# Gated DeltaNet layer of a two-layer backbone: the delta rule's scans issued in one order with both directions side by side, Q S in a PSUM bank of its own, 1/|k|² as a factor of a product, and the inverses' copies shared by two engines

## The chip, the cores and the metric

The kernel runs on one core of one Trainium2 chip. The metric is the device time of one execution in microseconds, the median of the runs shown. The kernel before took 1455.19 us (three runs, 1454.19 to 1458.78).

## The reference, cut to what matters

The network has two layers over 512 tokens (256 of context, 256 latent) of width 1024: a latent-attention layer with a SwiGLU channel mixer, then a bidirectional gated DeltaNet layer with a SwiGLU channel mixer. The change lies in the DeltaNet layer. Per value head and direction it computes, chunk by chunk:

```python
diff = gcum[..., :, None] - gcum[..., None, :]
decay = jnp.where(incl, jnp.exp(jnp.where(incl, diff, 0.0)), 0.0)
kb = kc * bc[..., None]
lmat = jnp.where(strict, jnp.einsum('bhnid,bhnjd->bhnij', kb, kc) * decay, 0.0)
a = lmat + jnp.eye(CHUNK, dtype=f32)
...
sol = lax.linalg.triangular_solve(a, rhs, left_side=True, lower=True, unit_diagonal=True)
attn = jnp.einsum('bhnid,bhnjd->bhnij', qc, kc) * decay
...
def step(S, inp):
    w_i, u_i, qd_i, kd_i, a_i, gl_i = inp
    v_new = u_i - jnp.einsum('bhck,bhkv->bhcv', w_i, S)
    o_i = jnp.einsum('bhck,bhkv->bhcv', qd_i, S) + jnp.einsum('bhij,bhjv->bhiv', a_i, v_new)
    S = S * gl_i[..., None, None] + jnp.einsum('bhck,bhcv->bhkv', kd_i, v_new)
    return S, o_i
```

The keys are divided by their norm before this. Both directions run over the context first and then over the latent tokens; only the latent output is used in this last layer.

## The kernel before, in words

**Work units.** The function `gdn` (L831) does the DeltaNet mixer. A unit n (0 to 7) is one key head with its two value heads e; a group g is two units. Tokens are cut into four chunks of 128 (0 and 1 context, 2 and 3 latent). The two directions d visit them in the orders (0, 1, 2, 3) and (1, 0, 3, 2).

**Steps.** `GDN_STEPS` (L71) is a hand-written table of some 70 words in which the steps are recorded: `keys`, `queries`, `values`, `gates` (projections from the layer input, streamed weights, a five-tap convolution on VectorE), `base` (the 32x32 diagonal blocks of the triangular matrices are inverted on GpSimd, one group at a time), `decays` and `invert` (one unit's triangular matrices and their inverses), `scan` (one unit's recurrence), `finish` or `last` (norm, gate and transpose of a unit's output) and `out` (the output projection, in parts). A scheduler then orders the instructions of each engine; steps in `URGENT` (L76), scans among them, get priority. An engine works its own list strictly in the order that comes out.

**decays (L1131).** For each direction a tile `N` of eight 128x128 blocks (chunk, value head) is loaded from `g_dram`, masked on GpSimd (L1147) and turned into decays by an Exp on ScalarE with the bias `nb` (L1149). `nb` holds the negative cumulated decay, less the logarithm of |k|²; this logarithm is made in `decay_factors` (L1020 to L1029) by two Newton steps on eight numbers per token row: per group 12 small VectorE instructions on the tiles `lnk`, `lnk_e`, `lnk_d` and `nb`, with two Exps between them. VectorE then multiplies with the products Q K (`at`, L1155, two instructions of 128x512 per unit) and K K (`N`, L1163, two instructions of 128x1024 per unit), both read from PSUM.

**invert (L1167).** The 32x32 inverses come by DMA. TensorE joins them to 64x64 blocks (`T` L1198, `Y` L1209 to L1211) and those to 128x128 (`T` L1220, `Y` L1226). Between the two rounds the results are copied from PSUM into `XA` and `N`: two copies on ScalarE (L1214) and four on VectorE (L1215, L1216); after the second round two on VectorE (L1228).

**scan (L1230).** A loop over four steps t, and in it over the two directions. In each: `ks` = K S (L1254) and, for latent chunks, Q S (L1256) into the other half of the same PSUM bank; `rr` (VectorE, L1259); `pw` = T rr (L1262); `w`, its copy (ScalarE, L1264); K^T w into the second half of the `pw` bank (L1268); the new state `S` (ScalarE at t = 0, VectorE afterwards, L1273); for latent chunks `av` (L1279) and the output `o` (L1284 to L1288). `ks` and `pw` take turns in two PSUM banks, called `ch`. Two further banks, `inv`, belong to decays and invert.

**Weights.** `Stream` loads weight tiles on SyncE's DMA queue (`raw`), splits each into `whi` (ScalarE, L185) and `wlo` (VectorE, L186), and three TensorE instructions use them (L213 to L215). These streamed products (`q`, `k`, `v`, `z`, `out`) are what the scheduler puts between the links of the scans.

Of the kernel before, what the change touches and what calls it, by code (L numbers as in the profile page):

```python
# [11 lines left out]
I32 = mybir.dt.int32  # L12
# [59 lines left out]
for _x in """keys0 base0 queries0 values0 keys1 base1 queries1 decays0 invert0 keys2 values1 decays1 invert1 queries2 gates1 base2 gates0 scan0 decays2 invert2 values2 scan1 scan2 decays3 gates2 invert3 values3 gates4 keys3 gates3 queries3 base3 finish0 scan3 decays4 invert4 gates5 values4 decays5 values5 values6 gates6 invert5 scan4 decays6 finish1 invert6 gates7 scan5 decays7 invert7 values7 out0 finish2 fetch0 scan6 out1 scan7 out2 out3 last6 out4 last7""".split():  # L72
    GDN_STEPS.append((_x[:-1], int(_x[-1])))
# [23 lines left out]
def tile_trunk(ctx: ExitStack, tc: tile.TileContext, xT, params, consts, gconsts, wmod, w0, w1, out):  # L97
# [15 lines left out]
    def bank(name="bank", tag="bank"):  # L113
        tags = env["tags"]
        if tag not in tags:
            tag = "bank" if "bank" in tags else "pj"
# [714 lines left out]
    def gdn(st, u, head, pool, big, fetch_base):  # L831
# [151 lines left out]
        def keys(g):  # L983
# [17 lines left out]
            ss, rk2 = tl([P, 8], "ss", 2), tl([P, 8], "rk2", 2)  # L1001
# [5 lines left out]
            groups[g] = dict(KT=KT, ss=ss, kk=kk)  # L1007

            def decay_factors():
# [8 lines left out]

                ln, ex, df = (tl([P, 8], n) for n in ("lnk", "lnk_e", "lnk_d"))
                V.tensor_scalar(ln, ss.bitcast(I32), math.log(2.0) / 2 ** 23, -math.log(2.0) * (127 - 0.043), op0=ALU.mult, op1=ALU.add)  # L1020
                for _ in range(2):
                    S.activation(ex, ln, AF.Exp)
                    V.tensor_tensor(df, ss, ex, op=ALU.subtract)
                    V.tensor_tensor(ex, ex, ss, op=ALU.add)
                    V.reciprocal(ex, ex)
                    V.tensor_tensor(df, df, ex, op=ALU.mult)
                    V.scalar_tensor_tensor(ln, df, 2.0, ln, op0=ALU.mult, op1=ALU.add)
                nb, bd = tl([P, 2, 2, 4, 2], "nb", 3), tl([P, 2, 2, 4, 2], "bd", 3)
                V.tensor_tensor(kc(nb), kc(ngc[:, :, gu]), wide(ln), op=ALU.subtract)  # L1029
                groups[g].update(nb=nb, bd=bd)  # L1030
# [67 lines left out]
        def values(n):  # L1098
            g, k = n // 2, n % 2
            s = groups[g]  # L1100
            Kt, Vt = tl([P, 4, P], "Kt", 1), tl([P, 4, 2, P], "Vt", 3)
# [20 lines left out]
            bd, Kb = s["bd"][:, :, k], tl([P, 2, 3, 2, P], "Kb", 2)  # L1122
# [8 lines left out]
        def decays(n):  # L1131
            if "nb" not in groups[n // 2]:
                flush()
            g, k = n // 2, n % 2
            s = groups[g]
            KT, QT, nb = s["KT"][:, k], s["QT"][:, k], s["nb"][:, :, k]
# [5 lines left out]
            for d in range(2):  # L1142
                for i in range(0, 8, 4):
# [4 lines left out]
                    for q in range(i, i + 4):  # L1148
                        S.activation(N[d][:, q], N[d][:, q], AF.Exp, bias=nb[:, d, q // 2, q % 2:q % 2 + 1])  # L1149
# [3 lines left out]
            at = tl([P, 2, 2, 2, P], "at", 2)  # L1153
            for d in range(2):
                V.tensor_tensor(at[:, d], qk[:, 0:TS].rearrange("p (c t) -> p c t", c=2).unsqueeze(2).to_broadcast([P, 2, 2, P]),  # L1155
                                N[d][:, 4:8].rearrange("p (c e) t -> p c e t", c=2), op=ALU.mult)
# [4 lines left out]
            for d in range(2):  # L1161
                x = N[d].rearrange("p (c e) t -> p c e t", e=2)
                V.tensor_tensor(x, kk.rearrange("p (c t) -> p c t", c=4).unsqueeze(2).to_broadcast([P, 4, 2, P]), x, op=ALU.mult)  # L1163
# [3 lines left out]
        def invert(n):  # L1167
# [22 lines left out]

            def qv(p, n):
# [20 lines left out]
            for d in range(2):  # L1212
                a0, b0, a1, b1 = tb[d]
                S.activation(X[B[b0], :, B[a0 % 2]], ps[d][B[b0]], AF.Copy)  # L1214
                V.tensor_copy(N[d][B[a0], :, B[b0]], ps[d][B[a0]])  # L1215
                V.tensor_copy(N[d][B[a1], :, B[b1]], ps[d][B[a1]])  # L1216
# [10 lines left out]
            for d in range(2):  # L1227
                V.tensor_copy(N[d][H[d], :, H[1 - d]], p[H[d]])  # L1228

        def scan(n):  # L1230
# [5 lines left out]
            KT, QT = s["KT"][:, k], s["QT"][:, k]  # L1236
            Sm = [tl([P, 2, P], "S", 4) for d in range(2)]
            o = tl([P, 2, 2, P], "o", 4)
            avb = bank("av", "av")
            av = avb.rearrange("p (c e n) -> p c e n", c=2, e=2)  # L1240
            opened = None
            for t in range(4):
                for d in range(2):
                    c = CHUNKS[d][t]
                    cs = slice(c * P, c * P + P)
                    Sk = Sm[d].rearrange("p e n -> p (e n)")
                    rr = Vt[:, c]

                    def tkn(x, e_):
                        return x[:, d, n, c, e_:e_ + 1]  # L1250

                    if t > 0:
                        ks = bank("ks", "ch")
                        PE.matmul(ks[:, :TS], KT[:, cs], Sk, start=True, stop=True)  # L1254
                        if c >= 2:
                            PE.matmul(ks[:, TS:], QT[:, (c - 2) * P:(c - 2) * P + P], Sk, start=True, stop=True)  # L1256
                        rr = tl([P, 2, P], "rr", 2)
                        for e_ in range(2):
                            V.scalar_tensor_tensor(rr[:, e_], ks[:, e_ * P:e_ * P + P], tkn(neg, e_), Vt[:, c, e_], op0=ALU.mult, op1=ALU.add)  # L1259
                    pw = bank("pw", "ch")  # L1260
                    for e_ in range(2):
                        PE.matmul(pw[:, e_ * P:e_ * P + P], N[d][:, 2 * c + e_], rr[:, e_], start=True, stop=True)  # L1262
                    w = tl([P, 2, P], "w", 3)
                    S.activation(w.rearrange("p e n -> p (e n)"), pw[:, 0:TS], AF.Copy)  # L1264
                    if t < 3:
                        kd = pw[:, TS:]
# [439 lines left out]
```

## Time and profile before

| | us |
|---|---|
| median of three runs | 1455.19 (1454.19 to 1458.78) |
| the profiled execution | 1455.09 |
| its span in the trace | 1453.3 |
| TensorE busy, share of the span | 1354.8 (93%) |
| VectorE busy | 990.0 (68%) |
| ScalarE busy | 734.7 (51%) |
| GpSimd busy | 221.4 (15%) |

The DeltaNet mixer fills the trace from about 695 to 1240 us. Before it lie the first layer and the mixer's first products, behind it the second channel mixer. In the profile's rows, "PE" is TensorE, "PEld" its weight loads, "DVE" VectorE, "ACT" ScalarE, "POOL" GpSimd and "SP" SyncE; "PEclk" is the share of TensorE's full clock that was granted in a stretch. A row of a table by stages reads: stretch, its length, busy time and count of each engine, granted clock, DMA share, GB/s. TensorE's busy time includes the modelled ends of its instructions, so a busy TensorE may still be waiting inside a chain of dependent products.

### The profile page before, as it was taken

What the parts mean: (1) busy time and instruction counts of PE and PEld (TensorE: products, weight loads), DVE (VectorE), ACT (ScalarE), POOL (GpSimd) and SP (SyncE); (2) the same over time, 40 slices, a digit from 0 to 9 for tenths busy, and PEclk for the clock granted to TensorE, in tenths of its full rate; (3) what the DMA queues carried; (4) which work ended last, traced back from release to release, by engine and by line L of the source; (5) the groups of instructions that cost most, each with busy time, mean ns of one, the idle gap of its engine ahead of it and who ended that gap; (6) DMA issues with size and microseconds to landing.
All of it is one profiled execution on the core that took longest, in us unless ns stands there. A gap on an engine that the chain in (4) does not pass through costs nothing. (4 is left out here: it accounts for less than half of the span.)

```text
span 1453.3 us, 27885 instructions
## 1 busy us (share of the span) xinstructions
PE 1354.8 (93%) x10753; PEld 1166.3 (80%) x10753; DVE 990.0 (68%) x2038; ACT 734.7 (51%) x1603; POOL 221.4 (15%) x329
## 2 busy tenths in 40 slices
PE   7999999999999999999797979889998998999996
PEld 4767687769989998987686858777877897899996
DVE  3355566979757956867789977667775765656665
ACT  3434444366524543542647645665566543745542
POOL 0000000050000000000017992934600000000000
PEclk9979999999999999999999989899999998899998
DMA  9444412654423332355146545433343243665551
GB/s 379 145 142 150 129 44 100 227 217 146 130 88 98 120 124 95 122 185 193 46 143 168 163 114 132 134 105 109 92 135 129 71 138 131 195 186 186 182 181 58
DMA packets 131692, 204.75 MB, mean 141 GB/s; under 512 B 70632, under 2 KB 72040, under 8 KB 131432
## 3 DMA queue, kind: packets, MB, share of 16 engines
q1 hardware_dynamic: 129656, 200.90, 43.3%
q10 hardware_dynamic: 1904, 2.08, 0.5%
q8 instruction: 84, 1.38, 0.4%
q14 instruction: 48, 0.39, 0.1%
HBM read 192.92 MB, written 10.03 MB: 140 GB/s over the span
## 5 line engine op out<-in xcount | busy, mean ns | idle before, releaser
L186 DVE TENSOR_TENSOR wlo<-raw,whi 128x512 fp32r<-128x512 f32 x422 | 295.7, 708 | 202.8 <-ACT whi L185 183.6
L185 ACT ACTIVATE whi<-raw 128x512 fp32r<-128x512 f32 x422 | 263.1, 630 | 322.1 <-PE ffo L214 71.5
L214 PE MATMUL ffo<-hidl,whi 128*128 128x512 f32 (+1 forms) x352 | 119.4, 339 | 0.0
L215 PE MATMUL ffo<-hidh,wlo 128*128 128x512 f32 (+1 forms) x352 | 119.2, 339 | 0.0
L213 PE MATMUL ffo<-hidh,whi 128*128 128x512 f32 (+1 forms) x352 | 118.9, 341 | 0.0
L185 ACT ACTIVATE whi<-wsum 128x512 fp32r<-128x512 f32 x88 | 54.9, 630 | 61.0 <-PE x L214 26.2
L1089 POOL TENSOR_TENSOR m<-m,mt 128x31 f32<-128x31 f32 (+15 forms) x124 | 79.1, 638 | 9.2
L1088 POOL TENSOR_TENSOR mt<-m 128x31 f32<-128x31 f32 (+15 forms) x124 | 77.1, 622 | 9.2
L213 PEld LDWEIGHTS ffo<-hidh,whi 128*128 128x128 f32 x352 | 66.9, 190 | 8.4 <-issue 0.7
L214 PEld LDWEIGHTS ffo<-hidl,whi 128*128 128x128 f32 x352 | 66.9, 190 | 8.0 <-issue 0.7
L215 PEld LDWEIGHTS ffo<-hidh,wlo 128*128 128x128 f32 x352 | 66.9, 190 | 7.6
L186 DVE TENSOR_TENSOR wlo<-wsum,whi 128x512 fp32r<-128x512 f32 x88 | 60.1, 689 | 15.8 <-ACT whi L185 15.5
L213 PE MATMUL z<-uhi,whi 128*128 128x256 f32 x216 | 62.9, 291 | 1.7 <-DVE acc L946 1.0
L215 PE MATMUL z<-uhi,wlo 128*128 128x256 f32 x216 | 62.8, 292 | 0.7 <-DVE wlo L186 0.7
L214 PE MATMUL z<-ulo,whi 128*128 128x256 f32 x216 | 61.9, 287 | 0.0
L213 PE MATMUL v<-uhi,whi 128*128 128x512 f32 x128 | 53.4, 417 | 7.3 <-ACT whi L185 4.6
L1177 POOL MEMSET XA<- 128x512 f32 x2 | 1.0, 525 | 364.0 <-PE modps L347 364.0
L1527 POOL TENSOR_TENSOR N<-N,mean 128x256 f32<-128x256 f32 x4 | 2.8, 722 | 332.8 <-DVE rs_t L247 332.8
L215 PE MATMUL v<-uhi,wlo 128*128 128x512 f32 x128 | 52.6, 412 | 0.7 <-DVE wlo L186 0.7
L560 POOL TENSOR_TENSOR r<-r,rstd 128x512 f32<-128x512 f32 x4 | 6.2, 1566 | 301.2 <-ACT rstd L549 300.3
L214 PE MATMUL v<-ulo,whi 128*128 128x512 f32 x128 | 52.0, 406 | 0.0
L213 PE MATMUL x<-t,whi 128*128 128x256 f32 x176 | 49.6, 282 | 0.1
(481 smaller groups left out, 4296.2 us busy)
## 6 DMA issues: line engine op xcount, KB each, us to landing
raw<-in_w_dram SPq DMA_DIRECT2D x153, 512.0 KB, 3.7
mraw<-in_wmod_dram SPq DMA_DIRECT2D x80, 512.0 KB, 5.4
raw<-in_w_dram SPq DMA_DIRECT2D x138, 256.0 KB, 2.9
raw<-in_wmod_dram SPq DMA_DIRECT2D x32, 256.0 KB, 4.5
N<-g_dram SPq DMA_DIRECT2D x16, 512.0 KB, 4.5
x<-in_xT_dram SPq DMA_DIRECT2D x4, 512.0 KB, 10.2
h<-in_xT_dram SPq DMA_DIRECT2D x1, 2048.0 KB, 9.3
m<-g_dram SPq DMA_DIRECT2D x16, 128.0 KB, 4.9
```

What stands on the lines that cost most here:

```text
L185: S.activation(hi, src, AF.Copy)
L186: V.tensor_tensor(lo, src, f32(hi), op=ALU.subtract)
L213: PE.matmul(ps_ap, a[0], b[0], start=first, stop=False, **kw)
L214: PE.matmul(ps_ap, a[0], b[1], start=False, stop=False, **kw)
L215: return PE.matmul(ps_ap, a[1], b[0], start=False, stop=last, **kw)
L560: (V if fb < 4 else G).tensor_tensor(r[fb], r[fb], rs if fb == 0 else f, op=ALU.mult)
L1088: G.tensor_tensor(tv, m[:, 0:j, j:j + 1].to_broadcast([P, j, w]), m[:, j:j + 1, j:32].to_broadcast([P, j, w]), op=ALU.mult)
L1089: G.tensor_tensor(m[:, 0:j, j:32], m[:, 0:j, j:32], tv, op=ALU.subtract)
L1177: G.memset(X, 0.0)
L1527: G.tensor_tensor(res.r[fb], res.r[fb], ms, op=ALU.subtract)
```

## The change

Five things are changed in the DeltaNet mixer; the table of steps is the same.

1. The logarithm of |k|² goes. The Exp takes the cumulated decay alone as its bias, and 1/|k|² (`rk2`, there already) is multiplied in on VectorE together with Q K and K K: `times`, one instruction per direction and chunk. Per unit there are four of 128x256 for `at` and eight for `N`, instead of two of 128x512 and two of 128x1024.
2. Between the rounds of invert, all copies of direction 0 are on VectorE and all of direction 1 on ScalarE.
3. The scan has both directions in each step, half a bank each: both K S into one `ks` bank, both Q S into a bank `qs` of the `inv` pair, then `rr`, `pw` and `w` of both, the state of both, the output of both.
4. Each TensorE instruction of a scan is issued after the one before it in the scan's own text (`mm` with `after(tail[0])`). The helper `fill` would put a step's generator between them; the table names no such step (no word with a "+"), so it does nothing here.
5. More buffers for `rk2`, `Vt`, `Kb`, `rr` and `w`, and a smaller scratch area for dynamic DMAs.

```diff
-                ln, ex, df = (tl([P, 8], n) for n in ("lnk", "lnk_e", "lnk_d"))
-                V.tensor_scalar(ln, ss.bitcast(I32), math.log(2.0) / 2 ** 23, -math.log(2.0) * (127 - 0.043), op0=ALU.mult, op1=ALU.add)
-                for _ in range(2):
-                    S.activation(ex, ln, AF.Exp)
-                    V.tensor_tensor(df, ss, ex, op=ALU.subtract)
-                    V.tensor_tensor(ex, ex, ss, op=ALU.add)
-                    V.reciprocal(ex, ex)
-                    V.tensor_tensor(df, df, ex, op=ALU.mult)
-                    V.scalar_tensor_tensor(ln, df, 2.0, ln, op0=ALU.mult, op1=ALU.add)
...
-                        S.activation(N[d][:, q], N[d][:, q], AF.Exp, bias=nb[:, d, q // 2, q % 2:q % 2 + 1])
+                        S.activation(N[d][:, q], N[d][:, q], AF.Exp, bias=ngc[:, d, n, q // 2, q % 2:q % 2 + 1])
...
+            def times(dst, c, d, x):
+                e2 = N[d][:, 2 * c:2 * c + 2]
+                V.scalar_tensor_tensor(dst, e2, rk2[:, c:c + 1], x.unsqueeze(1).to_broadcast([P, 2, P]), op0=ALU.mult, op1=ALU.mult)
...
+            def copy(d, dst, src):
+                V.tensor_copy(dst, src) if d == 0 else S.activation(dst, src, AF.Copy)
...
-                S.activation(X[B[b0], :, B[a0 % 2]], ps[d][B[b0]], AF.Copy)
-                V.tensor_copy(N[d][B[a0], :, B[b0]], ps[d][B[a0]])
-                V.tensor_copy(N[d][B[a1], :, B[b1]], ps[d][B[a1]])
+                copy(d, X[B[b0], :, B[a0 % 2]], ps[d][B[b0]])
+                copy(d, N[d][B[a0], :, B[b0]], ps[d][B[a0]])
+                copy(d, N[d][B[a1], :, B[b1]], ps[d][B[a1]])
...
+            def mm(*args, **kw):
+                with after(tail[0]):
+                    tail[0] = PE.matmul(*args, **kw)
+                return tail[0]
...
+                if t > 0:
+                    ks = bank("ks", "ch")
+                    for d, c in enumerate(cs):
+                        mm(half(ks, d), KT[:, c * P:c * P + P], Sk[d], start=True, stop=True)
+                    if t >= 2:
+                        qs = bank("qs", "inv")
+                        for d, c in enumerate(cs):
+                            mm(half(qs, d), QT[:, (c - 2) * P:(c - 2) * P + P], Sk[d], start=True, stop=True)
+                    else:
+                        fill()
```

In the scan every TensorE instruction of the changed kernel bears the line of `mm`, L1247. Where the instructions stand now is shown at three places.

VectorE's list before, in front of the copies of unit 0's first joined blocks (`N<-Y`); `lnk` and `nb` are the logarithm of group 1, which unit 0 does not need:

```order
L1174 STREAM_TRANSPOSE xb<-yb 128x256
L1025 RECIPROCAL lnk_e<-lnk_e 128x8
L1026 TENSOR_TENSOR lnk_d<-lnk_d,lnk_e 128x8
L1174 STREAM_TRANSPOSE yb<-xb 128x256
L1027 SCALAR_TENSOR_TENSOR lnk<-lnk_d,lnk 128x8
L1023 TENSOR_TENSOR lnk_d<-ss,lnk_e 128x8
L1024 TENSOR_TENSOR lnk_e<-lnk_e,ss 128x8
L1025 RECIPROCAL lnk_e<-lnk_e 128x8
L1026 TENSOR_TENSOR lnk_d<-lnk_d,lnk_e 128x8
L1027 SCALAR_TENSOR_TENSOR lnk<-lnk_d,lnk 128x8
L1029 TENSOR_TENSOR nb<-ngc,lnk 128x32
L186 TENSOR_TENSOR wlo<-raw,whi 128x512 x2
```

The same place now, with the copies themselves at the end (`rk_8532` is 1/|k|² of group 1):

```order
L1165 STREAM_TRANSPOSE xb<-yb 128x256
L1005 RECIPROCAL rk_8532<-ss 128x8
L1038 COPY ssq<-ss 128x8
L1165 STREAM_TRANSPOSE yb<-xb 128x256
L1020 TENSOR_TENSOR bd<-beta,rk_8532 128x32
L1006 TENSOR_TENSOR kkc<-kkd,rk_8532 128x256
L1183 COPY XA_7342<-Y_8290 32x8x32
L1183 COPY N<-Y_8290 32x8x32 x2
```

The ten rows of the logarithm and two splits of weights no longer stand ahead of the copies, and three copies stand there instead of four.

TensorE's list before, in the last two steps of the last scan (unit 7), where `out` is the streamed output projection:

```order
L1268 MATMUL pw<-w,Kb 128x128 x2
L1279 MATMUL av<-w,at 128x128 x2
L215 MATMUL out<-uhi,wlo 128x256
L1262 MATMUL pw<-rr,N 128x128 x2
L1254 MATMUL ks<-S,KT 128x256
L1256 MATMUL ks<-S,QT 128x256
L1268 MATMUL pw<-w,Kb 128x128 x2
L1279 MATMUL av<-w,at 128x128 x2
L1262 MATMUL pw<-rr,N 128x128 x2
L1254 MATMUL ks<-S,KT 128x256
L1256 MATMUL ks<-S,QT 128x256
```

The last scan now, from its second step on:

```order
L1247 MATMUL ks<-S,KT 128x256 x2
L1247 MATMUL pw<-rr,N 128x128 x4
L1247 MATMUL pw<-w,Kb 128x128 x4
L1247 MATMUL ks<-S,KT 128x256 x2
L1247 MATMUL qs<-S,QT 128x256 x2
L1247 MATMUL pw<-rr,N 128x128 x4
L1247 MATMUL pw<-w,Kb 128x128 x4
L1247 MATMUL av<-w,at 128x128 x4
L1247 MATMUL ks<-S,KT 128x256 x2
L1247 MATMUL qs<-S,QT 128x256 x2
```

The directions no longer alternate, and streamed products no longer stand between the links: from the first to the last `pw` of unit 7 there are 154 instructions of `out` in the list before and 19 now. The rest stands behind the scan: behind the last `pw` come 221 instructions of `out` now, 96 before.

TensorE's list now, where unit 4's `K K` product (`kk`) and its first joining product (`T`, which reads the finished `N`) stand, at the end of scan 3:

```order
L1247 MATMUL pw_10977<-rr_10969,N_9930 128x128 x2
L1151 MATMUL kk_11032<-KT_8384 128x128 x4
L1247 MATMUL av_10878<-w_10975,at_9963 128x128 x2
L1192 MATMUL T32_11055<-xb_11046,N_10992 32x32 x2
L1192 MATMUL T32_11055<-xb_11046,N_10994 32x32 x2
```

Only two products stand between `kk` and `T` now; before, the rows of most of a scan and of streamed `v` products stood between them.

More of the change, by code (lines that the diff above doesn't have):

```diff
@@ L115, in bank @@
         if tag not in tags:
-            tag = "bank" if "bank" in tags else "pj"
+            tag = next(t for t in ("bank", "ch", "pj") if t in tags)
         return env["ps"].tile([P, 512], F32, name=name, tag=tag, bufs=tags[tag])
@@ L1227, in invert, with drain, scan @@
             for d in range(2):
-                V.tensor_copy(N[d][H[d], :, H[1 - d]], p[H[d]])
-        def scan(n):
+                copy(d, N[d][H[d], :, H[1 - d]], p[H[d]])
+        def drain(steps):
+            for _ in steps:
+                pass
+        def scan(n, beside=()):
             if units[n].get("turned") != 1:
@@ L1236, in scan @@
             KT, QT = s["KT"][:, k], s["QT"][:, k]
+            beside, tail = iter(beside), [None]
             Sm = [tl([P, 2, P], "S", 4) for d in range(2)]
+            Sk = [x.rearrange("p e n -> p (e n)") for x in Sm]
             o = tl([P, 2, 2, P], "o", 4)
@@ new lines, in fill, with half, tkn @@
+            def fill():
+                for _ in range(2):
+                    with after(tail[0]):
+                        tail[0] = next(beside, tail[0])
+            def half(x, d):
+                return x[:, d * TS:d * TS + TS]
+            for t in range(4):
+                cs = [CHUNKS[d][t] for d in range(2)]
+                def tkn(x, d, e_):
+                    return x[:, d, n, cs[d], e_:e_ + 1]
+                rr = [Vt[:, c] for c in cs]
+                if t > 0:
[8 more added lines that the diff above has]
+                        fill()
+                    for d, c in enumerate(cs):
+                        rr[d] = tl([P, 2, P], "rr", 4)
@@ new lines, in scan @@
+                if t < 2:
+                    fill()
+                    continue
+                first = t == 2
+                for d, c in enumerate(cs):
+                    for e_ in range(2):
+                        opened = mm(av[:, c - 2, e_], at[:, d, c - 2, e_], ws[d][:, e_], start=opened is None, stop=not first, skip_group_check=True)
+                        q_ = half(qs, d)[:, e_ * P:e_ * P + P]
+                        if first:
+                            S.activation(o[:, c - 2, e_], q_, AF.Copy, scale=tkn(egc, d, e_))
+                        else:
+                            V.scalar_tensor_tensor(o[:, c - 2, e_], q_, tkn(egc, d, e_), o[:, c - 2, e_], op0=ALU.mult, op1=ALU.add)
+                    if not first:
+                        V.tensor_tensor(o[:, c - 2], o[:, c - 2], av[:, c - 2], op=ALU.add)
@@ L1289, in scan @@
+            drain(beside)
             un["o"] = o
@@ L1335, in project @@
                         ins = ob[m // 2][1] = first
+                    yield first
                 if k1 == 16 and m % 2:
@@ L1344, in gates @@
             for i in range(2):
-                ins = product(p[:, i * TS:i * TS + TS], upl, ins)
+                for k, x in enumerate(upl):
+                    with after(ins):
+                        ins = mm3(p[:, i * TS:i * TS + TS], st.take(), x, k == 0, k == NB - 1)
+                    yield ins
+                flush(ins)
             th, zt = tl([P, T], "th", 3), tl([P, 2, TS], "zt", 2)
@@ L1587, in _layer1_blocks @@
     ms = []
-    for step, i in GDN_STEPS:
+    for step, i in (x for steps in GDN_STEPS for x in steps):
         if step == "keys":
```

92 lines of the change are left out of this document (36 added, 56 removed).

## The prediction

> **What bounds the kernel now.** I read the page's first lines, then a table of the mixer by stages, then the waits of TensorE, the timelines at two places, and the groups of VectorE and ScalarE. The page gives the engines' shares of the span of 1453.3 us:
>
> ```profile
> PE 1354.8 (93%) x10753; PEld 1166.3 (80%) x10753; DVE 990.0 (68%) x2038; ACT 734.7 (51%) x1603; POOL 221.4 (15%) x329
> ```
>
> TensorE is the bound on the whole, so only its idle time and its throttled time can be won. By stages (the rows start with stretch and length, then TensorE's busy time, and end with granted clock, DMA share and GB/s):
>
> ```profile
> 840.00:873.00 33.00, 23.37 (x308) 19.59 (x308) 28.75 (x57) 15.32 (x36) 29.93 (x38) 0.84 0.46 111
> 873.00:1007.00 134.00, 121.73 (x1372) 104.30 (x1371) 96.99 (x236) 78.48 (x223) 61.21 (x107) 0.94 0.45 122
> 1007.00:1107.00 100.00, 95.23 (x966) 80.57 (x964) 72.10 (x151) 67.07 (x193) 36.86 (x58) 1.00 0.37 110
> 1107.00:1174.00 67.00, 60.09 (x782) 52.35 (x781) 40.95 (x102) 32.46 (x97) 1.22 (x2) 0.97 0.33 104
> 1174.00:1206.00 32.00, 30.18 (x232) 28.92 (x232) 20.88 (x58) 14.59 (x38) 0.00 (x0) 1.00 0.43 132
> 1206.00:1240.00 34.00, 26.05 (x158) 23.61 (x159) 21.35 (x63) 13.16 (x33) 0.00 (x0) 0.80 0.36 124
> ```
>
> The eight scans run from 873 to 1206. TensorE stands idle there for 12.27 + 4.77 + 6.91 + 1.82 = 25.8 us; no better order of the scans can win more. The stretch in front, with the first inverses (840 to 873), has 9.6 us idle and a clock of 0.84; the tail behind (1206 to 1240) has 8.0 us idle and 0.80. What lies before 695 and behind 1240 is not touched by the change; I put it at 0, give or take 4 us, an estimate, since the scheduler shifts a few products there.
>
> The sum is made against the profiled execution's own 1455.09 us, 0.1 us under the median.
>
> **Part A, the logarithm in front of unit 0's inverse.** The longest single wait of a join in 690 to 870, and VectorE's timeline around it (start, length):
>
> ```profile
> PE T L1220 <- DVE N L1216: 8.0, 1, 8.0
> ```
>
> ```profile
> 849.03 1.63 DVE L1026 TENSOR_TENSOR lnk_d<-lnk_d,lnk_e 128x8 f32<-128x8 f32 x1
> ...
> 855.22 1.76 DVE L186 TENSOR_TENSOR wlo<-raw,whi 128x512 fp32r<-128x512 f32 x2
> 856.91 0.41 DVE L1215 COPY N<-Y 32x256 f32<-32x256 f32 x1
> ```
>
> TensorE waits 8.0 us for copies that are ready to run but stand behind group 1's logarithm and two weight splits. In VectorE's list these rows are gone now. From 849.03 to 855.22 the logarithm takes 6.2 us, with small instructions of up to 1.63 us each in it. The splits (1.76) come later as well, and one of four copies (0.4) goes to ScalarE. Together 8.4 us leave the place, more than the wait, so what is late next there is TensorE's own work: 20 streamed `v` products now stand before `T`, which before mostly stood behind it. Cover used here is missing elsewhere, so I take −6, the logarithm alone; the ends are −8.0 (the whole wait) and −3 (half of the logarithm, if something else ends the wait). TensorE's granted clock was 0.84 over these 33 us, so 0.16 of 33 = 5.3 us of work were lost to the throttle. I leave that out of the sum, since the stretch has other waits than this one.
>
> [...]
>
> The logarithm's other cost is VectorE's time (two tiles of the chain, 690 to 1000; the first figure after the length is VectorE's):
>
> ```profile
> 690.00:1000.00 310.00, 11.52 (x32) 1.63 (x8) 0.93 0.46 124
> 690.00:1000.00 310.00, 4.89 (x16) 1.63 (x8) 0.93 0.46 124
> ```
>
> 16.4 us for 48 instructions; outside unit 0's place it lies beside TensorE's projections, and I count it at 0.
>
> **Part B, the scans.** The timeline inside one scan before:
>
> ```profile
> 1149.86 0.68 PE L1262 MATMUL pw<-rr,N 128*128 128x128 f32 x4
> ...
> 1150.58 0.38 ACT L1264 ACTIVATE w<-pw 128x256 f32<-128x256 f32 x1 [1.33 <-PE pw L1262]
> ...
> 1151.83 0.61 DVE L1273 SCALAR_TENSOR_TENSOR S<-S,egl,pw 128x128 f32<-128x128 f32 x2
> ...
> 1153.07 0.70 PE L1254 MATMUL ks<-S,KT 128*128 128x256 f32 x2
> ...
> 1154.24 0.61 DVE L1259 SCALAR_TENSOR_TENSOR rr<-ks,neg,Vt 128x128 f32<-128x128 f32 x2
> ```
>
> Before, `rr` could start only when Q S had been written into the same bank (1153.07 to 1154.24, 1.17 us); with Q S in its own bank it needs K S alone, 0.70. One direction's loop is `pw` to `w` 0.72, `w` through K^T w to `S` 1.25, `S` 0.61, K S 0.70, `rr` 0.61: 3.9 us, and with both directions in step nothing but this loop need bound a step. The groups (count | busy, mean ns | idle before, and for whom):
>
> ```profile
> L1259 DVE SCALAR_TENSOR_TENSOR rr<-ks,neg,Vt 128x128 f32<-128x128 f32 x96 | 29.1, 345 | 23.2 <-PE ks L1256 15.9 <-PE ks L1254 6.9
> L1163 DVE TENSOR_TENSOR N<-kk,N 128x1024 f32<-128x1024 f32 x16 | 19.1, 1215 | 0.0
> L1228 DVE COPY N<-Y 64x512 f32<-64x512 f32 x16 | 11.0, 686 | 3.2 <-PE Y L1226 3.0
> L1215 DVE COPY N<-Y 32x256 f32<-32x256 f32 x16 | 6.7, 416 | 0.8 <-ACT XA L1214 0.5
> L1288 DVE TENSOR_TENSOR o<-o,av 128x256 f32<-128x256 f32 x16 | 6.7, 416 | 6.7 <-PE av L1279 6.7
> L186 DVE TENSOR_TENSOR wlo<-raw,whi 128x512 fp32r<-128x512 f32 x175 | 126.9, 733 | 69.2 <-ACT whi L185 67.0 <-issue 0.9 <-PE k L214 0.5
> ```
>
> - `rr` waited 15.9 us for Q S. TensorE was busy with streamed products in part of that, so I take half: −8; the ends are 0 and −15.9. TensorE's 25.8 us of idle would hold either.
> - The products in `N` and `at` have 256 columns now. By `o`, of that size, one takes 0.42 us: per unit 8 x 0.42 = 3.4 for `N` in place of 2 x 1.215 = 2.4. (Those in `at` are read by the outputs `av` alone, at the end of a step: 0.) At unit 4 only two small products stand between `kk` and the join that needs `N`, so the 3.4 are open: +3.4. At the other units I take the difference of a quarter of a microsecond at most, +1.6. Together +5; the ends are 0 and 8 x 3.4 = +27, the last if no unit had cover.
> - Q S now takes a bank of the pair that decays and invert use. It may wait until VectorE or ScalarE has emptied `T` or `Y` from it; behind Q S on TensorE stand `pw` of both directions, and all of the scan waits for those. Such a release is one copy away (0.42 to 0.69 us). No row shows this wait; I take 0, between 0 and 24 x 0.69.
> - Copies: VectorE gives up two per unit of 0.42 and one of 0.69 and takes one of 0.42; ScalarE the reverse. Neither is near its limit over the scans (96.99 and 78.48 of 134 us in the first row), so 0. No DMA is added or moved, and SyncE's list is unchanged around the scans.
> - `fill` finds no step to put in, so it costs and brings nothing; the larger buffers allow the two directions' tiles to live at once.
>
> Part B: −8 + 5 = **−3**.
>
> **Part C, the tail.** Times at the end, from the chain of waits: first unit 7's first `pw`, then what follows its last, then (from TensorE's timeline) the first and the last of a run of streamed products between:
>
> ```profile
> 1174.44 0.71 PE pw L1262 x4
> ```
>
> ```profile
> 1203.16 0.76 PE pw L1262 x4
> ...
> 1213.13 0.64 PE oT L1318 x4
> 1215.26 0.74 PE out L213 x4
> ...
> 1222.06 0.43 PE lnmean L493 x2
> ```
>
> ```profile
> 1206.16 0.74 PE L213 MATMUL out<-uhi,whi 128*128 128x256 f32 x4 [1.01 <-ACT uhi L218]
> ...
> 1212.15 0.28 PE L215 MATMUL out<-uhi,wlo 128*128 128x256 f32 x1
> ```
>
> From 1206.16 to 1212.27 stand 48 `out`: 0.127 us each. Scan 7 takes 1174.44 to 1203.16 = 28.7 us from its first `pw` to its last, with 154 `out` in it. Without them the loop of Part B bounds it: 2.6 to the first state, two loops of 3.9, and 1.3 for the last K S and `rr` make 11.7; 0.6 for the second direction behind the first on VectorE, 1.0 for two outputs `o` ahead of an `rr`, and 19 x 0.127 = 2.4 for the `out` that stay make 15.7: −13.0. Ten more `out` stand in front: +1.3. Behind the last `pw`, 221 `out` in place of 96: the last state, `osq`, and the norm up to the transpose took 1203.16 to 1213.13; 145 `out` (18.4 us) cover them all now. Then 67 `out` follow up to the first `lnmean`, and they cover the wait from 1213.13 to 1215.26. So from the last `pw` to `lnmean` 212 x 0.127 + 1.2 for transposes and `av` = 28.1, where it was 1222.06 − 1203.16 = 18.9: +9.2. Sum −2.5. Part of the tail's throttled time (0.80 over 34 us) may go with the waits, −0.5. I take **−3**; the ends are −7 (the whole 8.0 us of idle goes, less the norm's chain behind `lnmean`) and +2 (the links of scan 7 cost 1 us a step more).
>
> **Sum.** 1455.09 − 6 − 3 − 3 = **1443 us**.
>
> **The rivals.**
> - *R1, slower: lockstep scans stand open.* The streamed products were what filled the links; fewer stand inside the later scans now, and VectorE works its list in order, so a weight split (0.733) can stand ahead of each `rr`, with both directions' `pw` behind it. On 24 steps that is 24 x 0.733 = +17.6 in Part B in place of −3. The sum is 1455 − 6 + 17.6 − 3 = 1464. It decides where Part B is over +9, and is measured as slower over +13.4. For it speak that TensorE has no second direction half a step away any more to work on, and that VectorE is 72% busy in the first scans; against it, that products displaced from a scan are not lost but shorten something else. Chance 0.23.
> - *R2, hidden.* The wait of Part A is only moved: VectorE's list gets shorter, but `v` waits for `whi` or its sums there, and scans win and lose alike: A −2, B 0, C 0, 1453. Range 1451 to 1459. Chance 0.18.
> - *R3, more.* All waits for Q S go (−16), the whole wait of unit 0 (−8), the tail −7: 1424. For it speaks that TensorE's idle time allows it; against it, that VectorE's list and TensorE's own work stand close behind each of these waits. Chance 0.13.
>
> **How the numbers follow.** The forecast holds 0.46: 1443. Its parts are open by about 3, 8 and 5 us, which seldom fall to one side together, so its own range is 1434 to 1451. A measurement of this kernel can tell about 0.3%, 4.4 us, from no change. Faster by more than that: forecast and R3, 0.46 + 0.13 = 0.59 (the upper end of the forecast's range lies at that border). Within: R2, 0.18. Slower: R1, 0.23. R3 lies between 1417 and 1434, R1 between 1460 and 1472 or so; the range of eight in ten takes in the nearer half of each, and leaves out 0.07 + 0.11: 1427 to 1465.
>
> **What would show it.** Part A: in the profile after, the wait of unit 0's second join (`T`, 64x64) for VectorE or ScalarE is under 2 us in place of 8.0, and the stretch from the first base inverses to the first scan is some 6 us shorter; it is wrong if a copy or a `v` sum is waited for as long. Part B: `rr` waits for K S and no longer for Q S; TensorE's idle time over the eight scans is near 23 us in place of 25.8; it is wrong if a row has TensorE waiting for `rr`, `w` or `S` with 20 us or more, which is R1, or for a bank of `qs`. The `N` products show if `T` of unit 4 waits over 3 us for VectorE. Part C: the last scan lies in 17 us, no wait before the last transpose, and `lnmean` follows its last `pw` by 28 us; wrong if the stretch from unit 7's first `pw` to the first `lnmean` is not about 4 us shorter than 47.6 (1174.44 to 1222.06). The whole prediction falls if the time is over 1451.

## The result and the profile after

The changed kernel takes 1464.63 us (median of four runs, 1462.81 to 1467.51), the kernel before 1455.33 in the same setting: a ratio of 1.0065, 95% interval 1.0044 to 1.0086. It is slower by about 9 us, where 1443 was forecast. 1464 was the price of the first rival; that is luck, since the mechanism of that rival is not what happened.

The page's row of the engines, after:

```profile
PE 1369.0 (94%) x10753; PEld 1177.1 (80%) x10753; DVE 980.5 (67%) x2038; ACT 742.4 (51%) x1611; POOL 223.2 (15%) x329
```

TensorE runs the same 10753 instructions and is "busy" 14 us longer. Busy counts a throttled instruction at its full length. Two equal products of the streamed `v` in the changed kernel's timeline show it, the first at half clock (0.50 granted from 1066.30 to 1071), the second at full clock (1.00 from 1072 to 1075.80):

```profile
1070.76 0.63 PE L214 MATMUL v<-ulo,whi 128*128 128x512 f32 x1
...
1073.41 0.39 PE L214 MATMUL v<-ulo,whi 128*128 128x512 f32 x1
```

The rest of the span did not grow (94.4 us in place of 98.5), so between these two executions the lost time is clock and not more waiting. The size is not the change's alone: the profiled execution of the kernel before had a mean granted clock of 0.963, near the top of that kernel's 0.951 to 0.965 over 29 runs (mean 0.958), the one of the changed kernel 0.953, like its other runs (mean 0.954).

In the two traces the first `w` of scan 0 comes 5.9 us earlier, the stretch from there to the first `w` of scan 7 is 20.4 us longer (321.1 in place of 300.7), and what follows is 4.4 us shorter. By stages, with bounds put at the first and last `w` of the scans:

```profile
868.00:913.00 45.00, 45.00 (x490) 39.94 (x490) 33.28 (x78) 33.51 (x90) 26.53 (x43) 1.00 0.55 139
913.00:957.00 44.00, 38.22 (x482) 33.70 (x480) 27.86 (x62) 23.23 (x65) 33.09 (x53) 0.88 0.43 130
957.00:989.00 32.00, 27.57 (x145) 22.06 (x146) 20.22 (x60) 15.64 (x49) 2.44 (x4) 0.95 0.19 55
989.00:1027.00 38.00, 36.85 (x402) 30.69 (x402) 31.20 (x76) 24.59 (x66) 6.07 (x15) 1.00 0.52 145
1027.00:1060.00 33.00, 29.82 (x201) 26.07 (x200) 21.77 (x47) 25.99 (x78) 29.79 (x42) 1.00 0.33 105
1060.00:1090.00 30.00, 22.82 (x296) 19.46 (x295) 21.32 (x50) 17.69 (x51) 6.51 (x17) 0.72 0.38 104
1090.00:1116.00 26.00, 23.62 (x328) 19.63 (x328) 13.10 (x39) 14.56 (x42) 0.00 (x0) 0.93 0.21 45
...
1122.00:1154.00 32.00, 30.97 (x375) 26.97 (x376) 16.62 (x42) 15.92 (x45) 0.00 (x0) 0.89 0.31 96
1154.00:1188.00 34.00, 32.92 (x380) 28.43 (x379) 21.80 (x64) 12.90 (x38) 0.00 (x0) 0.80 0.30 93
```

Two of these stages are no scan: 989 to 1027 (behind scan 2) and 1060 to 1090 (behind scan 3). Before, scans followed each other almost without a gap. In the first gap TensorE is busy (36.85 of 38 us, clock 1.00): it works off streamed `v` and `z` products. In the second the streamed work has run thin: 7.2 us idle, and a clock of 0.72, which by estimate, (1 − 0.72) x 30, takes 8.4 us. TensorE's timeline has 130 instructions of streamed products in the first gap, 42 in the second and 6 in scan 4 behind it (1090 to 1122). The scans themselves are shorter than before (317.5 us added up before, 259.0 now, from first to last `w`); the gaps between them add up to 79.5 us where they were 12.9.

What the gaps wait for stands in TensorE's timelines (start, length). Before: unit 3's product `K K` (`kk`), scan 2's first product (`pw<-Vt`), and unit 4's `kk`:

```profile
950.18 1.06 PE L1160 MATMUL kk<-KT 128*128 128x128 f32 x8
...
959.53 0.61 PE L1262 MATMUL pw<-Vt,N 128*128 128x128 f32 x4
...
1002.09 1.06 PE L1160 MATMUL kk<-KT 128*128 128x128 f32 x8
```

After, unit 3's and unit 4's, each behind the last Q S of a scan:

```profile
986.16 1.03 PE L1247 MATMUL qs<-S,QT 128*128 128x256 f32 x4
...
990.03 1.06 PE L1151 MATMUL kk<-KT 128*128 128x128 f32 x8
```

```profile
1054.65 1.03 PE L1247 MATMUL qs<-S,QT 128*128 128x256 f32 x4
...
1059.86 1.06 PE L1151 MATMUL kk<-KT 128*128 128x128 f32 x8
```

Unit 3's `kk` comes 40 us later than before, unit 4's 58 us. Before, unit 3's stood ahead of scan 2 and its inverse was built while scan 2 ran; now it starts when scan 2 has issued its last Q S. The reason, which the experiments below bear out, is the bank: `qk`, `kk`, `T`, `Y` and now `qs` take turns in the two banks `inv` in the order in which the program records them, and unit 3's decays and inverse are recorded behind scan 2, unit 4's behind scan 3. At both places the later user of the pair starts behind the earlier one, `kk` 3.9 and 5.2 us behind that Q S.

The delay reaches VectorE as well: the last group's `kkc`, which its base inverse on GpSimd needs, before and after:

```profile
978.98 0.42 DVE L1006 TENSOR_TENSOR kkc<-kkd,rk 128x256 f32<-128x256 f32 x1
```

```profile
1005.38 0.42 DVE L1006 TENSOR_TENSOR kkc<-kkd,rk 128x256 f32<-128x256 f32 x1
```

By TensorE's timelines its input `kkd` was done at 958 in both; what came later is VectorE's turn, in a list in which unit 3's products stand ahead of it now (`N<-N,rk,kk` at 994.69).

### The profile page after: what moved, and what is told of

Same layout as the page of the kernel before. It is cut to its first block, busy times and chain, and to the rows that moved or that the text cites. A ratio compares the mean times of both kernels' runs of the same rounds, so it can differ in the third digit from the quotient of the medians.

```text
span 1463.4 us, 27879 instructions
## 1 busy us (share of the span) xinstructions
PE 1369.0 (94%) x10753; PEld 1177.1 (80%) x10753; DVE 980.5 (67%) x2038; ACT 742.4 (51%) x1611; POOL 223.2 (15%) x329
## 4 chain that ended last, share of the span: by engine, by line
PE 70%; POOL 10%; DVE 5%; DMA 5%; issue 5%; ACT 4%; SPq 0%; ACTq 0%; POOLq 0%; DVEq 0%
PE ffo L214 4%; PE ffo L215 4%; POOL mt L1077 4%; PE ffo L213 4%; POOL m L1078 4%; PE x L213 3%; PE x L214 3%; PE x L215 3%; PE modps L347 3%; PE pw L1247 2%; DMA mraw<-in_wmod_dram 2%; PE pg L213 1%; PE y L213 1%; PE y L215 1%; ACT N L1136 1%
## 5 line engine op out<-in xcount | busy, mean ns | idle before, releaser
L186 DVE TENSOR_TENSOR wlo<-raw,whi 128x512 fp32r<-128x512 f32 x422 | 299.5, 716 | 217.8 <-ACT whi L185 200.0
L1077 POOL TENSOR_TENSOR mt<-m 128x31 f32<-128x31 f32 (+15 forms) x124 | 80.3, 648 | 9.3
L347 PE MATMUL modps<-mraw,cst 128*32 128x256 f32 x512 | 46.6, 424 | 4.2 <-DMA mraw<-in_wmod_dram 4.1
```

What stands on the lines that cost most here:

```text
L186: V.tensor_tensor(lo, src, f32(hi), op=ALU.subtract)
L347: PE.matmul(p[32 * b:32 * b + 32, 0:TS], cst[:, k], w[b], start=k == 0, stop=k == 7, tile_position=(0, 32 * b))
L1077: G.tensor_tensor(tv, m[:, 0:j, j:j + 1].to_broadcast([P, j, w]), m[:, j:j + 1, j:32].to_broadcast([P, j, w]), op=ALU.mult)
```

## The experiments

Each ran beside the kernel before, on four chips in all, so they are compared by their ratios; the medians of the kernel before there lie between 1456.47 and 1457.05 us. Theory 1: the bank, as above. Theory 2: scans side by side stand open by themselves (the first rival). Theory 3: the fixed order of TensorE's instructions costs.

**1. Q S beside K S again**

```diff
-                    ks = bank("ks", "ch")
                     for d, c in enumerate(cs):
-                        mm(half(ks, d), KT[:, c * P:c * P + P], Sk[d], start=True, stop=True)
+                        ks = bank("ks", "ch")
+                        mm(ks[:, :TS], KT[:, c * P:c * P + P], Sk[d], start=True, stop=True)
...
-                        qs = bank("qs", "inv")
+                            mm(ks[:, TS:], QT[:, (c - 2) * P:(c - 2) * P + P], Sk[d], start=True, stop=True)
```

The part of `o` that reads Q S is recorded ahead of `pw`, since the bank is wanted again.

> The changed kernel, with Q S put back beside K S, one bank of the scan's own pair per direction; both directions still go side by side, in the scan's fixed order, and the rest of the change stays. Theory 1 (the bank): Q S in the pair of decays and invert puts the next unit's K K and inverse behind the scan's last Q S; without that they stand inside the scan again, and the time falls by 12 us or more, to 1453 or less. Theory 2 (open links of the scans side by side): nothing of that changes, and rr waits for Q S again: 1465 to 1470. Theory 3 (the fixed order of TensorE's instructions): 1461 to 1468.

Measured: 1459.04 us, ratio 1.0023 (0.9998 to 1.0047). About 6 of the 9 us are gone, and the gaps between scans add up to 23.1 us (behind scans 2 and 3: 5.6 and 4.2). That is the direction of theory 1, but with half of the size that it expected.

**2. The bank alone**

```diff
-                            PE.matmul(ks[:, TS:], QT[:, (c - 2) * P:(c - 2) * P + P], Sk, start=True, stop=True)
+                            qs = bank("qs", "inv")
+                            PE.matmul(qs[:, :TS], QT[:, (c - 2) * P:(c - 2) * P + P], Sk, start=True, stop=True)
```

> The kernel before, with one edit: Q S of each direction goes to a bank of the pair of decays and invert. Directions in turn, no fixed order, logarithm and copies as before. Theory 1 (the bank): slower by 10 to 20 us, 1465 to 1475, with the last group's base inverse on GpSimd some 20 us later than 999.5. Theories 2 and 3: no scan side by side and no fixed order, and rr is free of Q S: 1447 to 1455.

Measured: 1462.63 us, ratio 1.0038 (1.0018 to 1.0058); `kkc` of the last group at 1008.78. The gaps behind scans 2 and 3 are 39.2 and 30.2 us, those of the changed kernel, with directions in turn and no fixed order. So the bank alone makes the gaps and costs 5 to 6 us, less than theory 1's 10 to 20; theories 2 and 3 had it no slower than before.

**3. No fixed order**

```diff
             def mm(*args, **kw):
-                with after(tail[0]):
-                    tail[0] = PE.matmul(*args, **kw)
-                return tail[0]
+                return PE.matmul(*args, **kw)
```

(`av` keeps the order that its accumulation needs.)

> The changed kernel without the fixed order: the scan's TensorE instructions are ordered by the scheduler, as far as data and banks leave it free. Theory 3 (fixed order): the loss of 9 us goes, 1450 to 1457. Theories 1 and 2: 1461 to 1468.

Measured: 1474.40 us, ratio 1.0129 (1.0098 to 1.0160). Without the fixed order it is slower by some 9 us: theory 3 falls, and neither of the others had foreseen the size. Gaps behind scans 2 and 3: 31.6 and 36.7.

**4. Parts 1 and 2 alone.** The kernel before with `times`, without the logarithm, and with the copies of the inverse by direction.

```diff
+                V.scalar_tensor_tensor(dst, e2, rk2[:, c:c + 1], x.unsqueeze(1).to_broadcast([P, 2, P]), op0=ALU.mult, op1=ALU.mult)
...
+                V.tensor_copy(dst, src) if d == 0 else S.activation(dst, src, AF.Copy)
```

> The kernel before with parts 1 and 2 of the change alone: 1/|k|^2 as a factor and no logarithm, the copies of the inverse on two engines; the scan is that of before. Theories 1, 2 and 3 all put the loss in the scan and leave Part A its 6 us: 1446 to 1451. A rival that puts the loss in the products of 256 columns gives 1458 or more.

Measured: 1449.22 us, ratio 0.9957 (0.9936 to 0.9978), −6.3 us. The whole loss lies in the rest of the change, the scan with its buffers: some 16 us between this kernel and the changed one.

**5. Q S in the transposes' bank**

```diff
-                        qs = bank("qs", "inv")
+                        qs = bank("qs", "tp")
```

> The changed kernel with one word changed: Q S takes the bank of the transposes (tp) and no longer the pair of decays and invert. Directions side by side, fixed order, all else as changed. Theory 1 (the bank; by the first runs it is 5 to 6 us of the loss): the K K products stand inside the scans again, some 6 us faster than the changed kernel, ratio to the kernel before 0.998 to 1.004. Theory 2 (the scans side by side cost by themselves, whatever bank): within 3 us of the changed kernel, 1.005 or more.

Measured: 1479.77 us, ratio 1.0162 (1.0136 to 1.0188). Both expectations missed. `K K` stood inside the scans again (unit 3's at 936.8, unit 4's at 985.2), yet the gaps behind scans 2 and 3 were 19.5 and 31.6 us. In this kernel's timeline of TensorE it is a transpose of the keys for a later unit that stands behind the last Q S of scan 2:

```profile
981.84 1.03 PE L1247 MATMUL qs<-S,QT 128*128 128x256 f32 x4
...
986.52 0.60 PE L1093 MATMUL kt<-ident,KT 128*128 128x128 f32 x4
```

The wait moved to the users of the other bank, `values`, of which a scan needs `Vt` and `Kb`. That reading comes from the timeline alone and was not tested further.

**6. Experiment 1 without the fixed order**

```diff
             def mm(*args, **kw):
-                with after(tail[0]):
-                    tail[0] = PE.matmul(*args, **kw)
-                return tail[0]
+                return PE.matmul(*args, **kw)
```

> The first experiment (directions side by side, Q S beside K S) without the fixed order. If going side by side costs by itself: as slow as that one or slower, ratio to the kernel before 1.002 or more. If it was the fixed order that cost there: near the kernel with parts 1 and 2 alone, 0.994 to 0.999.

Measured: 1457.92 us, ratio 1.0008 (0.9986 to 1.0029). This is 7 us above parts 1 and 2 alone, with the gaps small (26.8 us in all); the bound set for "side by side costs" was 1.002, so by its number it lies between the two expectations.

**7. Directions in turn, with a fixed order**

```diff
-                        PE.matmul(ks[:, :TS], KT[:, cs], Sk, start=True, stop=True)
+                        mm(ks[:, :TS], KT[:, cs], Sk, start=True, stop=True)
```

(and the same for every TensorE instruction of the scan, in the kernel of experiment 4)

> The kernel with parts 1 and 2 alone, directions in turn, with the scan's TensorE instructions chained in the order of the text. If the fixed order costs by itself: 6 us or more over that kernel, ratio to before 1.000 or more. If not: 0.993 to 0.998.

Measured: 1485.76 us, ratio 1.0195 (1.0168 to 1.0222), 35 us over experiment 4. The two largest of TensorE's waits there, in 868 to 1209, are links of the scan:

```profile
PE av L1239 <- ACT w L1264: 8.9, 7, 2.4
PE pw L1239 <- ACT w L1264: 6.9, 6, 2.8
```

The scans add up to 355.5 us (315.7 in experiment 4). With the two directions in turn the fixed order leaves these links open; with the directions side by side it was worth 9 us (experiment 3).

**8. Part 1 alone**, on the kernel before; the copies stay as they were.

```diff
-                        S.activation(N[d][:, q], N[d][:, q], AF.Exp, bias=nb[:, d, q // 2, q % 2:q % 2 + 1])
+                        S.activation(N[d][:, q], N[d][:, q], AF.Exp, bias=ngc[:, d, n, q // 2, q % 2:q % 2 + 1])
...
+                V.scalar_tensor_tensor(dst, e2, rk2[:, c:c + 1], x.unsqueeze(1).to_broadcast([P, 2, P]), op0=ALU.mult, op1=ALU.mult)
```

> The kernel before with part 1 alone (1/|k|^2 as a factor, no logarithm, products of 256 columns), copies as before. Part A of the prediction gives nearly all of the 6 us to this: ratio 0.994 to 0.997. If the copies on two engines brought the gain instead: 0.999 or more.

Measured: 1454.84 us, ratio 0.9983 (0.9968 to 0.9998), −2.5 us, between the two bounds. By the times 4 of the 6 us come with the copies on two engines, but the difference between the two runs is about as large as its uncertainty, and the trace does not bear it out (see Part A below).

**9. The bank in two scans alone**

```diff
+                            qs = bank("qs", "inv")[:, :TS] if n in (2, 3) else ks[:, TS:]
+                            PE.matmul(qs, QT[:, (c - 2) * P:(c - 2) * P + P], Sk, start=True, stop=True)
```

> The kernel before with Q S in the pair of decays and invert in scans 2 and 3 alone, all else as before. Theory 1 says that only these two cost, because unit 3's and unit 4's K K and inverse are recorded right behind them, and because the streamed products run out while they wait: the gaps between scans 2, 3 and 4 are 30 us or more, and the time is that of the run with all scans so, 1460 to 1465. If the bank cost a little in each scan: 1457 to 1459.

Measured: 1466.49 us, ratio 1.0064 (1.0040 to 1.0088), a little over the 1460 to 1465 expected. The bank in two scans is enough for a loss as large as the changed kernel's net loss of 9 us; it is not all of the 16 us that the scan's part lost. Unit 3's `kk` is behind scan 2's Q S again:

```profile
991.43 0.59 PE L1257 MATMUL qs<-S,QT 128*128 128x256 f32 x2
...
997.89 1.06 PE L1160 MATMUL kk<-KT 128*128 128x128 f32 x8
```

The gaps behind scans 2 and 3 are 34.9 and 32.3 us.

**10. The changed kernel, with other turns of the banks.** Only words of the table change places (the words in front and behind are the same and left out here):

```diff
-scan1 scan2 decays3 gates2 invert3 values3 gates4 keys3 gates3 queries3 base3 finish0 scan3 decays4 invert4 gates5
+scan1 decays3 invert3 scan2 gates2 values3 gates4 keys3 gates3 queries3 base3 finish0 decays4 invert4 scan3 gates5
```

> The changed kernel with the words of the table in another order: decays and invert of unit 3 are recorded ahead of scan 2, those of unit 4 ahead of scan 3; every instruction is kept. Theory 1: the bank's turns are then taken ahead of the scan's Q S, so K K of units 3 and 4 comes 30 us or more earlier, the gaps behind scans 2 and 3 fall from 38 and 30 us to under 10, and the time falls by 6 us or more, ratio to before at most 1.003. Theory 2 (side by side costs by itself, as in the first and sixth experiment) leaves it no better than the first experiment: 1.000 to 1.004. If neither: 1.005 or more.

Measured: 1443.26 us (1438.65 to 1446.63), ratio 0.9904 (0.9877 to 0.9931): 14 us faster than the kernel before and, by the ratios, 23 faster than the changed kernel, the fastest of all. TensorE's timeline has unit 3's `kk` ahead of both Q S of scan 2 now, and unit 4's `kk` ahead of scan 3, whose first `w` is at 1011.4:

```profile
961.97 1.06 PE L1151 MATMUL kk<-KT 128*128 128x128 f32 x8
...
981.73 1.13 PE L1247 MATMUL qs<-S,QT 128*128 128x256 f32 x4
...
994.11 1.03 PE L1247 MATMUL qs<-S,QT 128*128 128x256 f32 x4
...
997.96 1.13 PE L1151 MATMUL kk<-KT 128*128 128x128 f32 x8 [1.06 <-DVE rs_t L246]
```

The two `kk` come 28 and 62 us earlier than in the changed kernel (30 or more was expected). The gaps are 12.7 and 3.1 us, the first a little over the 10 expected, and `kkc` is back where it was:

```profile
979.20 0.42 DVE L1006 TENSOR_TENSOR kkc<-kkd,rk 128x256 f32<-128x256 f32 x1
```

The two rows by stages, first `w` of scan 0 to that of scan 7 and on to the second channel mixer's first product, of the kernel before, of the changed kernel and of this one:

```profile
874.00:1174.00 300.00, 276.06 (x3107) 236.22 (x3105) 209.04 (x485) 177.53 (x508) 98.45 (x164) 0.97 0.40 114
1174.00:1238.00 64.00, 54.52 (x385) 51.35 (x386) 40.23 (x116) 26.26 (x68) 0.00 (x0) 0.91 0.40 132
```

```profile
868.00:1189.00 321.00, 293.41 (x3130) 251.77 (x3130) 212.44 (x525) 188.86 (x533) 106.87 (x175) 0.91 0.38 109
1189.00:1248.00 59.00, 52.78 (x393) 49.19 (x391) 38.12 (x112) 24.51 (x63) 0.00 (x0) 0.95 0.40 134
```

```profile
870.00:1168.00 298.00, 278.40 (x3124) 241.38 (x3124) 211.98 (x524) 186.76 (x532) 107.73 (x178) 0.96 0.41 115
1168.00:1229.00 61.00, 54.71 (x399) 51.05 (x398) 38.51 (x114) 25.49 (x64) 0.00 (x0) 0.93 0.42 138
```

The same work takes 23 us less in the scans than in the changed kernel: TensorE's idle time falls from 27.6 to 19.6 us, and what the clock takes, by estimate, from (1 − 0.91) x 321 = 29 to (1 − 0.96) x 298 = 12 us. The kernel before has 23.9 us idle there and by the same estimate some 9 taken by the clock, so what the changed kernel lost in its scans is mostly clock.

**11. Side by side for units 6 and 7 alone**, in the kernel of experiment 4, with the changed kernel's scan as `scan_side` and its buffers for `rr` and `w`.

```diff
         def scan(n):
+            if n in (6, 7):
+                return scan_side(n)
```

> The kernel with parts 1 and 2 alone, and the changed scan (side by side, Q S in the pair of decays and invert, fixed order) for units 6 and 7 alone, behind which no inverse is recorded. Part C of the prediction is then had without the loss of the earlier scans: 2 to 4 us less than parts 1 and 2 alone, ratio to before 0.992 to 0.995. If side by side costs by itself also there: 0.996 or more.

Measured: 1450.18 us, ratio 0.9959 (0.9943 to 0.9975), no different from experiment 4 and between its two bounds. The gain expected of the tail alone did not appear. In the traces the tail is shorter (from unit 7's first `pw` to the first `lnmean` 45.3 us, in experiment 4 50.5), but the stretch from the first `w` of scan 0 to that of scan 7 is longer (301.8 against 297.6).

**12. Control: the table of experiment 10 on the kernel before**

```diff
-scan1 scan2 decays3 gates2 invert3 values3
+scan1 decays3 invert3 scan2 gates2 values3
...
-finish0 scan3 decays4 invert4 gates5
+finish0 decays4 invert4 scan3 gates5
```

> A control: the kernel before with the table of the tenth experiment and nothing else. If that run's gain of 23 us over the changed kernel is the removal of the bank's wait, this order brings the kernel before little, since its Q S takes no bank of the pair: ratio 0.997 to 1.003. If the order of the table is a gain of its own, whatever the bank: 0.990 to 0.995.

Measured: 1458.16 us, ratio 1.0013 (0.9997 to 1.0028); gaps 6.5 and 0.3 us, as before. The order of the table brings nothing by itself; of the two kernels in which it was tried, it pays in the one where Q S takes a bank of the pair.

The lengths of the scans and the gaps, from the first and last `w` of each scan in the traces (us):

| kernel | scans, sum | gap behind 2 | behind 3 | all gaps | ratio |
|---|---|---|---|---|---|
| before | 317.5 | 6.4 | 0.3 | 12.9 | 1 |
| changed | 259.0 | 37.9 | 29.8 | 79.5 | 1.0065 |
| 1: Q S beside K S | 313.0 | 5.6 | 4.2 | 23.1 | 1.0023 |
| 2: before, bank alone | 249.1 | 39.2 | 30.2 | 78.4 | 1.0038 |
| 3: no fixed order | 267.4 | 31.6 | 36.7 | 79.8 | 1.0129 |
| 4: parts 1 and 2 | 315.7 | 7.7 | 0.3 | 15.3 | 0.9957 |
| 9: bank in scans 2, 3 | 263.3 | 34.9 | 32.3 | 75.4 | 1.0064 |
| 10: other turns | 286.5 | 12.7 | 3.1 | 29.7 | 0.9904 |

## Why the prediction was wrong, point by point

**The step that failed** is the third point of Part B: "Q S now takes a bank of the pair that decays and invert use. It may wait until VectorE or ScalarE has emptied `T` or `Y` from it". It was priced at 0, between 0 and 24 x 0.69, by asking whom Q S waits for. It should have been asked the other way as well: who waits for Q S. Everything recorded behind the scan that uses the pair, for scans 2 and 3 the next unit's `qk`, `kk`, `T` and `Y`, stands behind the scan's last Q S. The rows needed were there: the pieces of TensorE's list shown ahead of the prediction had unit 4's `kk` in the last step of scan 3, and that was read as a price for the products in `N` (+3.4), not as an inverse that comes late (58 us, as the trace shows). In place of Part B's −3 the stretch of the scans, from the first `w` of scan 0 to that of scan 7, became 20.4 us longer. Experiments 2 and 9 make the same gaps, and a loss of 5 to 9 us, by this edit alone; experiment 10 takes the gaps and some 23 us away from the changed kernel. Why the same wait costs more in the changed scan than in the scan of before is not shown.

**Part A was right, and its size rather too small.** The 8.0 us wait of unit 0's second join is gone from TensorE's waits in 690 to 868, and the first `w` of scan 0 starts at 867.7 in place of 873.6, 5.9 us earlier. Counted from unit 0's `kk`, so that differences ahead of it drop out, that `w` comes 115.4 to 117.9 us later in the four traces with the logarithm and 105.0 to 109.4 us later in the ten without it: some 9 us apart, more than the forecast's 6. With part 1 alone (experiment 8) it is 105.0, so the logarithm makes this gain, as forecast, and the copies, put at 0, are not needed for it. Experiment 8 then takes 307.2 us from the first `w` of scan 0 to that of scan 7, where the kernel before takes 300.7, with TensorE less idle (17.8 against 24.2 us) and at a lower clock (0.94 against 0.97); so what its time lacks against experiment 4 was lost behind Part A's place. (The list of VectorE shown with the change has nine rows of the logarithm, not ten; the sum does not use their number.) The row of the clock around unit 0 moved to 0.88 over the stretch before the first scan:

```profile
840.00:868.00 28.00, 23.55 (x313) 20.03 (x314) 24.27 (x44) 14.10 (x30) 25.96 (x31) 0.88 0.63 143
```

By estimate, (1 − 0.88) x 28, that is 3.4 us lost in place of 5.3. The forecast had left this out of its sum; whether the 3 us by which the 9 exceed its 6 are of the clock the traces do not decide.

**Part B's other terms.** `rr` stopped waiting for Q S, as forecast, and its idle time fell from 23.2 to 10.0 us:

```profile
L1278 DVE SCALAR_TENSOR_TENSOR rr<-ks,neg,Vt 128x128 f32<-128x128 f32 x96 | 26.9, 342 | 10.0 <-PE ks L1247 9.7
L1143 DVE SCALAR_TENSOR_TENSOR N<-N,rk,kk 128x256 f32<-128x256 f32 x64 | 26.6, 471 | 4.3 <-PE kk L1151 4.3
L1143 DVE SCALAR_TENSOR_TENSOR at<-N,rk,qk 128x256 f32<-128x256 f32 x32 | 13.4, 471 | 0.0
```

The split products take 0.47 us in place of the 0.42 taken over from `o`. Their +5 was not seen: unit 4's first join waited 0.2 us for `N` (+3.4 was the price), and experiments 4 and 8 with them are faster, so this is not where the time went. (For the other units the prediction takes a quarter of a microsecond each, where its own figures, 3.4 and 2.4, differ by 1.0.) With the turns of the bank put right, the changed kernel is 14 us faster than before; the forecast's sum was −12. By the traces its three stretches, up to scan 0, to scan 7 and behind, are 3.8, 2.1 and 2.8 us shorter, 8.7 in all, in an execution at a lower clock than that of before (0.956 against 0.963), so each part is of the forecast's order, and the closeness of the two sums says no more than that.

**Part C.** From unit 7's first `pw` (1187.96) to its last (1205.44) it is 17.5 us, with 15.7 forecast, and from there to `lnmean`, by the chain of waits of the changed kernel:

```profile
1205.60 0.45 PE pw L1247 x4
1208.21 0.44 PE oT L1343 x4
...
1221.16 4.24 DMA raw<-in_w_dram
...
1233.57 0.43 PE lnmean L493 x2
```

28.1 us, as forecast. Together 45.6 in place of 47.6, 2.0 us shorter where about 4 were forecast; the 1.8 us that are missing lie in the scan. In the chain stands a weight load of 4.24 us, a wait that the prediction had not named. Experiment 11, which wanted this gain alone, did not measure it, so −3 is neither shown nor excluded. The −0.5 in it for throttled time that goes with the waits was the author's estimate; no run shows that term by itself. The granted clock behind the last `pw` was 0.94 (1205.60 to 1248), where the tail before had 0.80 (1206 to 1240).

**The first rival** hit the size by luck and not the mechanism. It had weight splits ahead of `rr` in every step, with TensorE waiting 20 us or more for `rr`, `w` or `S`; in 868 to 1206 these waits add up to some 10 us, `rr` waits less for K S and Q S now, the scans are shorter, and experiment 10 runs all of them side by side with a gain. What it had right is that streamed products are the cover: they are spent in the first gap, and the second has too few.

**The clock.** The second gap has 7.2 us of idle TensorE, 3.8 of them in one wait (unit 4's second join, from 1076.4 to 1080.2, for a copy into `XA` that the change moved to VectorE and the prediction put at 0), and a granted clock of 0.72. In the changed kernel's trace the half clock lies in these stretches, among others:

```profile
1065.00:1072.00 7.00, 6.21 (x27) 4.78 (x27) 1.50 (x3) 6.30 (x20) 2.37 (x5) 0.51 0.70 189
...
1079.00:1089.00 10.00, 8.12 (x83) 7.78 (x84) 9.45 (x18) 3.60 (x9) 0.00 (x0) 0.50 0.23 60
1160.70:1174.30 13.60, 13.60 (x184) 10.92 (x184) 8.87 (x32) 4.42 (x11) 0.00 (x0) 0.50 0.11 29
```

The second sets in during the wait of 3.8 us (0.68 granted from 1078 to 1080.10, 1.00 in the 2.2 us ahead of that). The first sets in behind pauses of at most 1.3 us, and the third behind one of 0.9, with TensorE's records busy throughout; so in this trace the half clock came behind short pauses as well as in a long one, and what sets it off is not shown. The prediction weighed the clock at Part A and at the tail, where waits went, and not at the places where waits could arise. How much of the loss is clock alone was not measured: no run holds the waits and changes the clock. The mean granted clock of the runs is 0.954 for the changed kernel, 0.9585 for before and 0.9615 for experiment 10, but 0.9585 for experiment 2 as well, which is 5 us slower at the clock of before.

**Still open.** Experiments 1 and 6 lie 7 to 10 us above parts 1 and 2 alone with small gaps. They put as many tiles of each step through the two banks `ch` as experiment 4 (two `ks`, two `pw`), but in another order, which may be the reason; this was not tried by itself. Why experiment 3 loses 9 us without the fixed order, where experiment 6 loses nothing against experiment 1, is open too.

## What to carry to other kernels

A tile that takes turns in a small pool is an order: ask not only what it waits for, but what is recorded behind it in the same pool and may no longer pass (here unit 4's `kk`, 58 us later). If an early step moves from the middle of a scan to behind it, read that in the order as lateness, and follow it to who needs it next. Where a resource's turns follow the order of the program text, moving a few words of that text may be worth more than the edit that caused the wait cost: here some 23 us against 9.

## What the runs showed of the hardware that was not expected

The runs of one kernel on one chip lie further apart than the forecast assumed: 29 runs of the kernel before went from 1446.90 to 1462.12 us, and the fastest had a mean granted clock of 0.965, the slowest one of 0.956. TensorE ran at half clock (0.50 granted) for 13.6 us in which its records are busy throughout (1160.70 to 1174.30), so a busy row can hide a throttle. A fixed order of the same instructions cost 35 us where two chains were in turn (experiment 7) and was worth 9 us where they went side by side (experiment 3 against the changed kernel).
